# One decoder layer on one core: a carried sum folded to 64 rows, projections dealt out by step size, and three reorderings

## The chip, the core and the metric

The kernel runs on one core of a Trainium2 chip. The core has a matrix engine (TensorE, PE in the profile, with its weight loads as PEld), three engines for elementwise work (VectorE or DVE, ScalarE or ACT, GpSimd or POOL), a sync engine SP that issues most DMAs, and 16 DMA engines. Each engine works through its own queue in order; semaphores tie the queues together. The metric is the device time of one execution in microseconds (us). Before the change the median of three runs is 848.81 us, from 848.63 to 849.54.

## The reference

One layer of a decoder on 512 tokens of width 1024, all in float32: a mixer, a cross-attention into 256 memory tokens, a feed-forward, and a last normalisation.

```
h = rms_norm(x, norm_mix);  proj = h @ w_in
q, k, v, u, gate_b, gate_c, g_a, g_b = split(proj)
# stick-breaking attention, 8 heads of 64, strictly causal
z = q.k / sqrt(64)
log_fail = where(mask, log_sigmoid(-z), 0)
log_later = reverse_cumsum(log_fail) - log_fail
o_a = where(mask, exp(log_sigmoid(z) + log_later), 0) @ v
y_b = gate_b * causal_conv3(gate_c * u)
x += (sigmoid(g_a) * (o_a @ w_branch_a) + sigmoid(g_b) * (y_b @ w_branch_b)) @ w_mix_out
x += memory_cross_attention(rms_norm(x), rms_norm(mem))     # 4 heads of 256
gate, up = split(rms_norm(x) @ w_ffn_in);  x += (silu(gate) * up) @ w_ffn_out
out = rms_norm(x, norm_final)
```

## The kernel before

**Numbers.** A float32 operand is split into a high and a low part of a shorter type: ScalarE copies (casts) the value to the high part, VectorE subtracts to get the low one. A product is then three matmuls (high·high, low·high, high·low; lines 154 to 156), and a projection of one 128-wide output tile over 512 tokens is 8 x 3 = 24 matmuls of 512 columns. Its weights arrive by a DMA on SP's queue (`wr`, line 141) and are split by ScalarE (`wh`, line 149) and VectorE (`wl`, line 150).

**The stick-breaking attention.** Four pairs of heads `p` are swept; for each the key tiles `kt` go 3, 2, 1, 0, so there are 16 steps `(p, kt)`. Key tile `kt` sees the queries from `128 kt` on: 128, 256, 384 and 512 columns a head. Scores stand transposed, keys on the 128 rows. A step has three parts:

- `scores(p, kt)` (line 437) makes z on PE; ScalarE and VectorE turn it into e, the softplus of z (lines 444 to 447), which GpSimd masks with a select (line 402). `fails` splits e into `l` (lines 416, 417), adds what the key tiles above left (line 462), and queues `rests`, which splits that running sum into two tiles `r`, high and low.
- `weights(p, kt)` adds to z the running sum over all rows of the later key tiles (matmuls with `neg1`, all −1, line 480; one for each part of `r`) and the sum within the tile (matmuls with `negtri`, line 483; one for each part of `l`). ScalarE takes the exponential (`a`, line 485), GpSimd masks it (line 402), and VectorE makes `ah` and `al` (lines 489, 490).
- `values` multiplies by v (line 502) and at kt = 0 joins the two heads' halves in `ot` (lines 510, 511).

**What sets the order.** The loop over the steps (line 554) deals out a list `fill` of projections for the next pair (`qk_part`), the convolution branch (`conv`: gc, cu and gb in turn, lines 372 to 388) and the first gates, so that PE has work while the other engines make e and a. Step i issues its fills, with the scores of step i+1 in their middle, then its own `weights`, then `values` of step i−1. The number of fills of a step follows a straight line through the whole list. Each engine gets its instructions in the order in which a scheduler then lays them. Before step 9 `mem_factors` is issued: it normalises the memory tokens' factors `rm`, writes them to DRAM (`rmd`, line 534) and reads them back spread over all rows (`rmb`, line 536), both by GpSimd's DMA queue:

```
d = dpool.tile([1, MEM], F32, tag="rm", name="rmd")
nc.gpsimd.dma_start(d.rearrange("o (t p) -> p (o t)", p=P), rm)
rmb = cpool.tile([P, MEM], F32, tag="rmb", name="rmb")
nc.gpsimd.dma_start(rmb, d.broadcast_to([P, MEM]))
```

**Later stages.** The merge (lines 613 to 636) makes eight tiles `merged[m]`, each split into `mh` and `ml` (line 174); the memory keys `km` follow (lines 635 to 648), evicted by VectorE at line 642 with `rmb`. The feed-forward forms its first product from seven products of half size in each of 22 column blocks, so a use `(m, i)` is product i of block m (line 855); the list `uses` is their order on PE. Products 0, 3, 4 and 5 of a block share one PSUM bank `z`, which is read between them (`sa`, `sb`, line 876, ScalarE); product 1 has bank `v`, products 2 and 6 have `y`. `mean2` and `turn_r2` (lines 1071 to 1076) give the feed-forward's normalisation; `second` is a VectorE addition behind product 4. At the end `last_half` multiplies the last 128 rows of output, and for them `rstd(t1)`, `rstd_end(t1)` and `store` normalise and write out (lines 1274 to 1309).

PSUM has two banks for projections, four for z and two for o; all short-lived tiles (`e`, `a`, `cu`, `ot`) share eight buffers.

Of the kernel before, what the change touches and what calls it, by code (L numbers as in the profile page):

```python
# [9 lines left out]
F32R = mybir.dt.float32r  # L10
AF = mybir.ActivationFunctionType
# [32 lines left out]
def hybrid_layer(ctx: ExitStack, tc: tile.TileContext, xT_d, memT_d, mem_d, cols_d, wv_d, win_d,  # L44
# [18 lines left out]
    def nm(s):  # L63
        count[0] += 1
        return f"{s}{count[0]}"
# [102 lines left out]
    def split(src, s, scale=None, cols=512, last=()):  # L168

        hi, lo = unit(s + "h", cols), unit(s + "l", cols)  # L170
        if scale is None:
            casts.append(nc.scalar.copy(hi, src))
            after(casts[-1], last)
            nc.vector.tensor_tensor(out=lo, in0=src, in1=f(hi), op=ALU.subtract)
        else:
            nc.scalar.activation(hi, src, AF.Copy, scale=scale)
            nc.vector.scalar_tensor_tensor(out=lo, in0=src, scalar=scale, in1=f(hi),
                                           op0=ALU.mult, op1=ALU.subtract)
        return hi, lo
# [234 lines left out]
    def lsplit(t, n, tag, bufs, last=()):  # L414
        hi, lo = (lpool.tile([P, n], F32R, tag=tag, name=nm(tag), bufs=bufs) for _ in range(2))
        after(nc.scalar.copy(hi, t), last)
        nc.vector.tensor_tensor(out=lo, in0=t, in1=f(hi), op=ALU.subtract)
        return hi, lo

    def rests(p, kt, hs, e, w, last):  # L420
        rest[p, kt - 1, hs] = lsplit(e, w, f"r{kt}", 4 // len(hs), last)

    def part_of(parts, hs, some, n):

# [118 lines left out]
        fill += [(conv, p, i) for i in range(3)]  # L543
    for m in range(EARLY):
        fill += [(gate, m, 0), (gate, m, 1)]
    n_fill = len(fill)

    qk_part(0, 0)
    qk_part(0, 1)
# [4 lines left out]
    for i in range(len(steps) + 1):  # L554
        if i in MEM_AT:
            mem_square(MEM_AT.index(i))
        if i == MEAN_AT:
            rm, rmb = mem_factors()
        some = []
        while fill and (n_fill - len(fill) < (i + 1) * (n_fill - 1) / len(steps)  # L560
                        if i < len(steps) else True):
            some.append(fill.pop(0))
        if i + 1 < len(steps):
            to = lambda: scores(*steps[i + 1])
            if len(some) == 1:
# [46 lines left out]
    for m in range(KD):  # L612
        sig = []
        for j in range(2):
            if (m, j) not in gates:
                gate(m, j)
            t = gates.pop((m, j))
            sigmoid = nc.scalar.activation(t, t, AF.Sigmoid)
            after(sigmoid, exps[-2:])
            sig.append(t)  # L620
        w = load_w(wbr_d[m])
        for j in (1, 0):
            if m == 0 and j == 0:
                gate(EARLY, 0)
            ps = mmtile("br")
            gemm(ps, w, (oT, yb)[j], 4 * j)
            nc.vector.tensor_tensor(out=sig[j], in0=ps, in1=sig[j], op=ALU.mult)
        nc.vector.tensor_tensor(out=sig[0], in0=sig[0], in1=sig[1], op=ALU.add)
        merged.append(split(sig[0], "m"))
        if m == SUMS_AT:  # L630
            weight_sums(range(SUMS_FIRST), merged[m][0])
        if m % 2 == 0:
            mem_split(m // 2)
# [3 lines left out]
    for m in range(KD):  # L637
        w = load_w(wmk_d[m])
        ps = mmtile("km")
        gemm(ps[:, :MEM], w, mg)  # L640
        t = tmp("km", MEM)
        nc.vector.tensor_tensor(out=t, in0=ps[:, :MEM], in1=rmb, op=ALU.mult)
        if m % 2 == 0:
            pair = unit("kmh"), unit("kml")
        hi, lo = (u[:, (m % 2) * MEM:(m % 2 + 1) * MEM] for u in pair)
        nc.scalar.copy(hi, t)
        nc.vector.tensor_tensor(out=lo, in0=t, in1=f(hi), op=ALU.subtract)
        km.append((hi, lo))
    vm = [[None] * 2 for _ in range(MT)]
    for n in range(2):  # L650
        pss = [ztile("vm") for _ in range(MT)]
# [254 lines left out]
                n1 = acts[j][1][:, :HS]  # L906
                nc.vector.tensor_tensor(out=n1, in0=acts[j][0][:, :HS], in1=n1, op=ALU.subtract)

    uses = [(0, 0), (0, 1), (0, 2)]
    for m in range(NF):  # L910
        if m < NF - 2:
            uses += [(m, 3), (m + 1, 0), (m, 4), (m + 1, 1), (m, 5), (m + 1, 2), (m, 6)]
        elif m == NF - 2:
            uses += [(m, 3), (m + 1, 0), (m, 4), (m + 1, 1), (m + 1, 2), (m + 1, 3), (m, 5),
                     (m + 1, 4), (m, 6), (m + 1, 5), (m + 1, 6)]
# [135 lines left out]
    with tc.manual_schedule(engines={mybir.EngineType.PE, mybir.EngineType.Activation,  # L1051
# [6 lines left out]
        for n, (m, i) in enumerate(uses):  # L1058
            if (m, i) == (1, 0):
                product(banks[m]["z"], m, i, range(KP - 1, KP))  # L1060
            elif n > 2:
                product(bank_of(m, i), m, i)
            if i == 4:
                reads(m, i)
            else:
                if i == 1 and m > 0:
                    second(m - 1)
                reads(m, i)
            if n + AHEAD < len(uses):
                ffn_form(*uses[n + AHEAD])  # L1070
            if n + AHEAD + SUM_AHEAD < len(uses):
                ffn_raw(*uses[n + AHEAD + SUM_AHEAD])
            if (m, i) == (1, 1):
                mean2 = mean2()
            elif (m, i) == (0, 6):
                r2b[0] = mean2[0]("r0b", bank=mmtile)
                turn_r2()

            if i == 0 and m > 1:
                evict(m - 2, 0)  # L1080
            elif i == 4 and 0 < m < NF - 1:
                evict(m - 1, 1)
            elif i == 1 and m > 1:
                evict(m - 2, 2)
            if (m, i) == (NF - 2, 6):
                w, x3 = out_cast(*w23(0)), half_form(3, 0, 0)
                evict(m, 0)
                evict(m, 1)
                rest_of(*x3)
                x2 = half_form(2, 1, 0)  # L1090
            if (m, i) == (NF - 1, 5):
                evict(NF - 2, 2)
                rest_of(*w)
                rest_of(*x2)
                n2_of(x2[0], 1)
                x3 = half_form(3, 1, 0)
            if n == len(uses) - 6:
                w, x = out_cast(*w01(0)), cast_first(0)
                rest_of(*w)
                rest_of(*x)  # L1100
            elif (m, i) == (NF - 1, 4):
                w, x = out_cast(*w01(1)), cast_first(1)
                x2 = half_form(2, 0, 0)
                second(NF - 1)
                rest_of(*w)
                rest_of(*x)
                rest_of(*x2)
                n2_of(x2[0], 0)
# [165 lines left out]
        def rstd(ts):  # L1274


            a, b = ss[:, :TT][:, ts], ss[:, TT:][:, ts]
            if ts == t1:
                nc.vector.tensor_scalar(out=var[:, ts], in0=b, scalar1=a, scalar2=s1b, op0=ALU.add,
                                        op1=ALU.add)  # L1280
            else:
                nc.vector.tensor_tensor(out=var[:, ts], in0=a, in1=b, op=ALU.add)
            after(nc.scalar.activation(ry[:, ts], var[:, ts], AF.Ln, bias=eps_t), tables)
            nc.scalar.activation(ry[:, ts], ry[:, ts], AF.Exp, scale=-0.5)
            nc.vector.tensor_scalar(out=rv[:, ts], in0=var[:, ts], scalar1=EPS, scalar2=None,
                                    op0=ALU.add)

        def rstd_end(ts):

# [11 lines left out]
        def store(t, h, how):  # L1301
            y, r = ys[t, h], ra[:, t:t + 1]
            if how == "act":
                nc.scalar.activation(y, y, AF.Copy, scale=r)
            else:
                nc.vector.scalar_tensor_tensor(out=y, in0=y, scalar=r, in1=gain[h], op0=ALU.mult,
                                               op1=ALU.mult)
            q = nc.scalar if (t, h) == (1, 0) else nc.sync
            q.dma_start(out[t * P:(t + 1) * P, h * 512:(h + 1) * 512], y)

        def last_half(c):
            bank = ztile("p5b")
# [23 lines left out]
        rstd_end(t0)  # L1336
        half()
        store(0, 0, "act")
        half = last_half(1)
        store(0, 1, "both")  # L1340
        half()
        rstd(t1)
        rstd_end(t1)
        store(1, 1, "both")
        store(1, 0, "act")


_OUT = ((512, 1024), 'float32')
# [61 lines left out]
```

## Time and profile before

| what | us |
|---|---|
| median of three runs | 848.81 (848.63 to 849.54) |
| the profiled execution, its own time | 848.86 |
| its span, first to last instruction | 847.2 |
| PE busy | 837.0 |
| VectorE busy | 654.0 |
| ScalarE busy | 453.3 |
| GpSimd busy | 158.9 |

The page divides the span into busy time of each engine; the chain that ended last follows the work back from the last instruction; the list of waits says which engine stood idle for whom; and the timeline gives single instructions with their start, their duration and, in brackets, the idle time before them and what ended it. Matmuls overlap: one of 512 columns is shown as 390 ns, though the next starts after some 227, so distances between starts are what counts on PE. In a row, `out<-in` names the tiles, and `xN` counts instructions that the view has merged.

### The profile page before, as it was taken

To read this page: it belongs to the slowest core of one execution; us is meant where nothing else is said; L and a number is where in the kernel's file an instruction comes from. 1 tells how busy PE (TensorE), PEld (TensorE's weight loads), DVE (VectorE), ACT (ScalarE), POOL (GpSimd) and SP (SyncE) were. 2 spreads that over 40 slices of the span, in tenths; PEclk is the share of its full clock that TensorE was granted. 3 is DMA by queue.
4 is the path that set the end of the run, shared out by engine and by line. 5 is a ranking of instruction groups with operands and counts; after the bars stand their busy time and mean duration, and the time that the engine had idled before them with its cause. 6 is when DMAs were issued, how large, how long until landed. Compare 5 with 4: busy or idle time off the path is not lost.

```text
span 847.2 us, 12667 instructions
## 1 busy us (share of the span) xinstructions
PE 837.0 (99%) x4779; PEld 737.9 (87%) x4779; DVE 654.0 (77%) x1036; ACT 453.3 (54%) x806; POOL 158.9 (19%) x165
## 2 busy tenths in 40 slices
PE   9999999999999999999999999999999999999996
PEld 7888887888888899888888789999999999988885
DVE  7878978895757686588455689888888778899886
ACT  7576766574333344443444556655555555666654
POOL 0011121220556660163000001111111110000401
PEclk9999999999999999999999999999999999999999
DMA  8552454225588776466431425767767773465552
GB/s 299 158 159 100 131 103 97 80 78 188 195 306 306 268 267 200 171 227 250 152 83 50 111 74 144 177 179 182 191 177 187 190 186 86 149 223 200 179 182 99
DMA packets 51214, 143.72 MB, mean 170 GB/s; under 512 B 5745, under 2 KB 6769, under 8 KB 48338
## 3 DMA queue, kind: packets, MB, share of 16 engines
q1 hardware_dynamic: 41506, 107.89, 38.5%
q0 software_dynamic: 9360, 34.75, 15.7%
q8 instruction: 37, 0.61, 0.3%
q10 hardware_dynamic: 288, 0.28, 0.1%
q14 instruction: 23, 0.19, 0.1%
HBM read 125.20 MB, written 13.64 MB: 164 GB/s over the span
## 4 chain that ended last, share of the span: by engine, by line
PE 95%; DVE 2%; ACT 1%; issue 1%; POOL 0%; POOLq 0%; DVEq 0%; ACTq 0%
PE z L855 15%; PE p L1124 12%; PE y L855 7%; PE pr L154 7%; PE pr L155 7%; PE pr L156 7%; PE v L855 4%; PE r L155 3%; PE r L154 3%; PE r L156 3%; PE v L272 3%; PE mq L156 2%; PE mq L154 2%; PE mq L155 2%; PE br L156 2%; PE br L155 2%
## 5 line engine op out<-in xcount | busy, mean ns | idle before, releaser
L149 ACT CAST wh<-wr 128x1024 fp32r<-128x1024 f32 x84 | 88.0, 1051 | 156.5 <-issue 65.5
L150 DVE TENSOR_TENSOR wl<-wr,wh 128x1024 fp32r<-128x1024 f32 x84 | 112.4, 1340 | 36.5 <-ACT wh L149 35.9
L154 PE MATMUL pr<-xgh,wh 128*128 128x512 f32 x288 | 112.9, 392 | 0.1
L155 PE MATMUL pr<-xgl,wh 128*128 128x512 f32 x288 | 112.4, 390 | 0.0
L156 PE MATMUL pr<-xgh,wl 128*128 128x512 f32 x288 | 112.2, 390 | 0.0
L589 POOL TENSOR_TENSOR pre<-pre 128x512 f32<-128x512 f32 x44 | 73.7, 1679 | 31.7 <-DMA pre<-in_w_ffn_out_dram 29.4
L824 POOL DMA_DIRECT2D ws<-in_w_ffn_in_dram x22 | 26.6, 1210 | 256.1 <-DVE wf L845 120.2
L855 PE MATMUL z<-xdh,wf 128*128 128x256 f32 x352 | 70.4, 283 | 0.0
L156 PEld LDWEIGHTS pr<-xgh,wl 128*128 128x128 f32 x288 | 54.1, 188 | 11.5
L154 PEld LDWEIGHTS pr<-xgh,wh 128*128 128x128 f32 x288 | 54.1, 188 | 10.9 <-DVE gc L372 0.3
L155 PEld LDWEIGHTS pr<-xgl,wh 128*128 128x128 f32 x288 | 54.1, 188 | 10.5
L876 ACT COPY sa<-z 128x256 f32<-128x256 f32 x44 | 16.4, 372 | 79.2 <-PE z L855 79.1
L855 PEld LDWEIGHTS z<-xdh,wf 128*128 128x128 f32 x352 | 58.0, 192 | 0.0
L845 DVE TENSOR_TENSOR wf<-s,wf 128x512 fp32r<-128x512 f32 x44 | 30.3, 690 | 25.9 <-ACT wf L844 25.7
L855 PE MATMUL z<-xdl,wf 128*128 128x256 f32 x176 | 49.8, 283 | 0.0
L936 DVE TENSOR_TENSOR wl<-wr,wh 128x1024 fp32r<-128x1024 f32 x33 | 41.0, 1243 | 4.7 <-ACT wh L1003 4.7
L1003 ACT CAST wh<-wr 128x1024 fp32r<-128x1024 f32 x33 | 34.6, 1049 | 5.5 <-PE xt L1209 2.8
L855 PE MATMUL z<-xch,wf 128*128 128x256 f32 x176 | 35.4, 284 | 0.1
L855 PE MATMUL v<-xoh,wf 128*128 128x256 f32 x176 | 35.4, 283 | 0.0
L855 PE MATMUL y<-xch,wf 128*128 128x256 f32 x176 | 35.4, 283 | 0.0
L855 PE MATMUL z<-xf,wf 128*128 128x256 f32 x264 | 35.4, 283 | 0.0
L855 PE MATMUL y<-xoh,wf 128*128 128x256 f32 x176 | 35.3, 283 | 0.0
(341 smaller groups left out, 2391.8 us busy)
## 6 DMA issues: line engine op xcount, KB each, us to landing
wr<-in_w_in_dram SPq DMA_DIRECT2D x36, 512.0 KB, 3.3
pre<-in_w_ffn_out_dram POOLq DMA_DIRECT2D x11, 1024.0 KB, 8.0
sums<-pre POOLq DMA_DIRECT2D x11, 1024.0 KB, 5.0
ws<-in_w_ffn_in_dram SPq DMA_DIRECT2D x22, 512.0 KB, 3.7
wg<-in_w_ffn_in_dram SPq DMA_DIRECT2D x22, 512.0 KB, 4.3
ws<-in_w_ffn_in_dram POOLq DMA_DIRECT2D x22, 512.0 KB, 6.3
wr<-sums SPq DMA_DIRECT2D x22, 512.0 KB, 3.8
wr<-in_w_ffn_out_dram SPq DMA_DIRECT2D x16, 512.0 KB, 3.8
```

The source lines that it names most:

```text
L149: after(nc.scalar.copy(h2, raw), lead[-1:])
L150: lows.append(nc.vector.tensor_tensor(out=l2, in0=raw, in1=f(h2), op=ALU.subtract))
L154: nc.tensor.matmul(ps, a[0], b[0], start=start, stop=False, **kw)
L155: nc.tensor.matmul(ps, a[0], b[1], start=False, stop=False, **kw)
L156: nc.tensor.matmul(ps, a[1], b[0], start=False, stop=stop, **kw)
L589: nc.gpsimd.tensor_tensor(out=t[:, a, :], in0=t[:, a, :], in1=t[:, b, :], op=ALU.add)
L824: nc.gpsimd.dma_start(s13, a[:, 0:4:3, :], accum_op=ALU.add)
L845: nc.vector.tensor_tensor(out=w[:, 1, :], in0=raw, in1=f(w[:, 0, :]), op=ALU.subtract)
L855: nc.tensor.matmul(ps[:, :HS], a, b, start=i < 3 and k == 0 and j == 0, stop=k == KP - 1 and j == 2, skip_group_check=True)
L936: nc.vector.tensor_tensor(out=lo, in0=src, in1=f(hi), op=ALU.subtract)
L1003: nc.scalar.copy(hi, raw)
L1124: nc.tensor.matmul(res[i][s2], a[:, ts], b, start=j == 0 and n == 0, stop=n == 2 and j == (BEHIND - 1 if (i, s2) == (5, 1) else NJ - 1))
```

## The change

Six edits:

1. `rests` no longer splits the running sum into two tiles of 128 rows. It adds the upper 64 rows to the lower 64 (ScalarE copies the upper half to a temporary's lower rows, VectorE adds), and puts the high part of the result into rows 0 to 63 of one tile and the low part into rows 64 to 127. `weights` then needs one matmul with `neg1` instead of two.
2. The loop deals two fills to each step with kt = 1 and one to each other step, and the rest at the end.
3. The split of the last merged tile is issued behind the eviction of `km[0]`.
4. The first uses of the feed-forward come in another order; `second(0)`, `mean2` and `turn_r2` move with them.
5. For the last 128 rows Ln takes the last partial sum of squares `s1b` as its input and the rest as its bias, so the sum isn't formed first.
6. The last two stores are issued from a function of their own: ScalarE's half first, VectorE's half in two pieces.

```diff
     def rests(p, kt, hs, e, w, last):
-        rest[p, kt - 1, hs] = lsplit(e, w, f"r{kt}", 4 // len(hs), last)
+        low, high = HALVES
+        t = tmp("rf")[:, :w]
+        after(nc.scalar.copy(t[low, :], e[high, :]), last)
+        nc.vector.tensor_tensor(out=t[low, :], in0=t[low, :], in1=e[low, :], op=ALU.add)
+        r = lpool.tile([P, w], F32R, tag=f"r{kt}", name=nm("r"), bufs=2 // len(hs))
+        nc.scalar.copy(r[low, :], t[low, :])
+        nc.vector.tensor_tensor(out=r[high, :], in0=t[low, :], in1=f(r[low, :]), op=ALU.subtract)
+        rest[p, kt - 1, hs] = r,
...
-        while fill and (n_fill - len(fill) < (i + 1) * (n_fill - 1) / len(steps)
-                        if i < len(steps) else True):
+        while fill and (i == len(steps) or len(some) < (2 if steps[i][1] == 1 else 1)):
             some.append(fill.pop(0))
...
-        merged.append(split(sig[0], "m"))
+        if m < KD - 1:
+            merged.append(split(sig[0], "m"))
...
         km.append((hi, lo))
+        if m == 0:
+            merged.append(split(sig[0], "m"))
...
-    uses = [(0, 0), (0, 1), (0, 2)]
-    for m in range(NF):
+    uses = [(0, 0), (0, 1), (0, 2), (0, 3), (1, 0), (1, 1), (0, 4), (1, 2), (0, 5), (0, 6)]
+    for m in range(1, NF):
...
-                if i == 1 and m > 0:
+                if i == (2 if m == 1 else 1) and m > 0:
                     second(m - 1)
...
-            if (m, i) == (1, 1):
+            if (m, i) == (0, 5):
                 mean2 = mean2()
-            elif (m, i) == (0, 6):
+            elif (m, i) == (1, 3):
...
+        def rstd_begun(ts):
+            nc.vector.tensor_scalar(out=var[:, ts], in0=ss[:, :TT][:, ts],
+                                    scalar1=ss[:, TT:][:, ts], scalar2=EPS, op0=ALU.add,
+                                    op1=ALU.add)
+
+        def rstd_of_rest(ts):
+            nc.scalar.activation(ry[:, ts], s1b, AF.Ln, bias=var[:, ts])
+            nc.scalar.activation(ry[:, ts], ry[:, ts], AF.Exp, scale=-0.5)
+            nc.vector.tensor_tensor(out=rv[:, ts], in0=var[:, ts], in1=s1b, op=ALU.add)
...
+        def store_last(t):
+            r = ra[:, t:t + 1]
+            rows = out[t * P:(t + 1) * P, :]
+            nc.scalar.activation(ys[t, 0], ys[t, 0], AF.Copy, scale=r)
+            nc.scalar.dma_start(rows[:, :512], ys[t, 0])
+            for c in range(2):
+                cs = slice(c * HS, (c + 1) * HS)
+                y = ys[t, 1][:, cs]
+                nc.vector.scalar_tensor_tensor(out=y, in0=y, scalar=r, in1=gain[1][:, cs],
+                                               op0=ALU.mult, op1=ALU.mult)
+                nc.sync.dma_start(rows[:, 512 + c * HS:512 + (c + 1) * HS], y)
...
+        rstd_begun(t1)
         half = last_half(1)
         store(0, 1, "both")
         half()
-        rstd(t1)
+        rstd_of_rest(t1)
         rstd_end(t1)
-        store(1, 1, "both")
-        store(1, 0, "act")
+        store_last(1)
```

In the changed kernel the lines of `weights` are 8 higher (480 is 488, 483 is 491, 502 is 510, 534 is 542, 536 is 544).

**PE, step 9, weights(2,2).** Its rows before: scores of the next step, then a whole projection (`pr314`, 24 matmuls, of which the first two and the last are shown), then the matmuls with the carried `l3` and with `l2` into bank `z282`, then values.

```order
L437 MATMUL z308_1421<-qk187_889,qk205_969 128x384
L154 MATMUL pr314_1442<-xgh21_153,wh312_1438 128x512
L155 MATMUL pr314_1442<-xgl22_154,wh312_1438 128x512
...
L156 MATMUL pr314_1442<-xgh47_218,wl313_1439 128x512
L480 MATMUL z282_1305<-l3272_1270,neg1_91 128x2x128
L480 MATMUL z282_1305<-l3273_1271,neg1_91 128x2x128
L483 MATMUL z282_1305<-l2291_1352,negtri_95 128x512
L483 MATMUL z282_1305<-l2292_1353,negtri_95 128x512
L502 MATMUL o320_1483<-ah286_1335,v63_351 128x128
```

The same place in the changed kernel: the scores stand in the middle of the one projection that is left in this step (`pr305`, the last 12 of its 24 matmuls follow, the first and the last of them are shown).

```order
L445 MATMUL z307_1413<-qk187_891,qk205_971 128x384
L154 MATMUL pr305_1397<-xgh35_188,wh303_1393 128x512
...
L156 MATMUL pr305_1397<-xgh47_218,wl304_1394 128x512
L488 MATMUL z282_1309<-l3272_1274,neg1_91 128x2x128
L488 MATMUL z282_1309<-l3273_1275,neg1_91 128x2x128
L491 MATMUL z282_1309<-l2291_1356,negtri_95 128x512
L491 MATMUL z282_1309<-l2292_1357,negtri_95 128x512
L510 MATMUL o314_1453<-ah286_1339,v63_351 128x128
```

The projection `pr314` has moved behind weights(2,2).

**POOL and VectorE at the same place, in the changed kernel.** First GpSimd: the write of `rm`, the mask of the scores' e, the reading back, the mask of a of the step before, and the next masks.

```order
L542 DMA rmd_1387<-rm301_1380 128x2x1
L402 AFFINE_SELECT e283_1314<-e283_1314 128x2x128
L544 DMA rmb_1389<-rmd_1387 128x256
L402 AFFINE_SELECT a285_1336<-a285_1336 128x256
L402 AFFINE_SELECT a311_1446<-a311_1446 128x2x128
```

Up to the fourth of these rows nothing has moved against before; the fifth then stood two masks later. VectorE behind that mask of a (`a285`), up to `l2292`, which the second matmul L491 above reads, and on to the new add of the fold (`rf296`):

```order
L497 TENSOR_SCALAR ah286_1339<-a285_1336,r071_372 128x256
L519 TENSOR_TENSOR ot288_1347<-o221_1048,ot288_1347 64x512
L498 SCALAR_TENSOR_TENSOR al287_1340<-a285_1336,r071_372,ah286_1339 128x256
L519 TENSOR_TENSOR ot288_1347<-o222_1049,ot288_1347 64x512
L417 TENSOR_TENSOR l2292_1357<-e283_1314,l2291_1356 128x512
L470 TENSOR_TENSOR e283_1314<-e283_1314,e264_1230 128x2x128
L174 TENSOR_TENSOR ol290_1353<-ot288_1347,oh289_1352 128x512
L336 TENSOR_TENSOR qk294_1362<-qk284_1332,qk293_1361 128x512
L425 TENSOR_TENSOR rf296_1369<-rf296_1369,e283_1314 64x512
```

The first five of these rows stand in the same order as before.

**VectorE, the last merged tile.** Before, with `ml` ahead of the eviction of the first `km`:

```order
L150 TENSOR_TENSOR wl616_3010<-wr614_3007,wh615_3009 128x1024
L174 TENSOR_TENSOR ml594_2895<-g582_2822,mh593_2894 128x512
L642 TENSOR_TENSOR km599_2929<-km598_2904,rmb_1383 128x256
L150 TENSOR_TENSOR wl621_3045<-wr619_3042,wh620_3044 128x1024
L647 TENSOR_TENSOR kml601_2932<-km599_2929,kmh600_2931 128x256
```

and in the changed kernel:

```order
L150 TENSOR_TENSOR wl616_3018<-wr614_3015,wh615_3017 128x1024
L649 TENSOR_TENSOR km597_2933<-km596_2908,rmb_1389 128x256
L150 TENSOR_TENSOR wl621_3053<-wr619_3050,wh620_3052 128x1024
L654 TENSOR_TENSOR kml599_2936<-km597_2933,kmh598_2935 128x256
L174 TENSOR_TENSOR ml601_2940<-g582_2830,mh600_2939 128x512
```

The split `ml` has moved behind the eviction, the next weights' subtract and the split of `km`.

More of the change, by code (lines that the diff above doesn't have):

```diff
@@ L545, in hybrid_layer @@
         fill += [(gate, m, 0), (gate, m, 1)]
-    n_fill = len(fill)
     qk_part(0, 0)
@@ L1277, in rstd @@
             a, b = ss[:, :TT][:, ts], ss[:, TT:][:, ts]
[L1278 to L1282, printed above, removed]
+            nc.vector.tensor_tensor(out=var[:, ts], in0=a, in1=b, op=ALU.add)
             after(nc.scalar.activation(ry[:, ts], var[:, ts], AF.Ln, bias=eps_t), tables)
@@ L1307, in store @@
                                                op1=ALU.mult)
-            q = nc.scalar if (t, h) == (1, 0) else nc.sync
-            q.dma_start(out[t * P:(t + 1) * P, h * 512:(h + 1) * 512], y)
+            nc.sync.dma_start(out[t * P:(t + 1) * P, h * 512:(h + 1) * 512], y)
+        def store_last(t):
[9 more added lines that the diff above has]
+                nc.sync.dma_start(rows[:, 512 + c * HS:512 + (c + 1) * HS], y)
         def last_half(c):
```

## The prediction

> **What bounds the kernel now.** I read the page's busy shares first, then the chain that ended last, then what TensorE waited for.
>
> ```profile
> PE 837.0 (99%) x4779; PEld 737.9 (87%) x4779; DVE 654.0 (77%) x1036; ACT 453.3 (54%) x806; POOL 158.9 (19%) x165
> PE 95%; DVE 2%; ACT 1%; issue 1%; POOL 0%; POOLq 0%; DVEq 0%; ACTq 0%
> PE warm L232 <- DVE neg L91: 1.4, 1, 1.4
> PE z L437 <- ACT a L485: 0.9, 1, 0.9
> PE km L154 <- DVE km L642: 0.3, 1, 0.3
> 731.03 62.59 PE p L1124 x276
> ```
>
> TensorE (PE) is the bound: 837.0 of 847.2 us, 95% of the chain, and only three waits of note. So two kinds of edit can pay: fewer matmul columns, and the removal of a wait of PE itself. Any wait that the change adds to PE counts in full. The last row gives the true rate: 276 matmuls of 512 columns in 62.59 us, **0.227 us each** (a matmul's own duration overlaps the next), so a projection of 24 takes 5.44 us. Everything below is by start to start.
>
> **Folded rests.** In each head pair, 2 of 4 neg1 matmuls of 256 columns and 2 of 4 of 384 columns go. Their groups, and PE's timeline where they stand:
>
> ```profile
> L480 PE MATMUL z<-r,neg 128*128 128x384 f32 x16 | 4.1, 335 | 0.0
> L480 PE MATMUL z<-r,neg 128*128 128x256 f32 x16 | 3.2, 279 | 0.0
> ...
> 134.57 0.40 PE L480 MATMUL z<-l,neg 128*128 128x256 f32 x2
> 134.80 0.62 PE L483 MATMUL z<-l,negtri 128*128 128x512 f32 x2
> ...
> 151.24 0.51 PE L480 MATMUL z<-r,neg 128*128 128x384 f32 x2
> 151.58 0.62 PE L483 MATMUL z<-l,negtri 128*128 128x512 f32 x2
> ```
>
> Two of 256 columns occupy 134.80 − 134.57 = 0.23 us, two of 384 columns 151.58 − 151.24 = 0.34 us. Half of each sixteen goes: 4 x 0.23 + 4 x 0.34 = **−2.28 us**. In exchange each of 12 rests gets one ScalarE copy and one VectorE add more, on 64 rows.
>
> ```profile
> L511 DVE TENSOR_TENSOR ot<-o,ot 64x512 f32<-64x512 f32 x8 | 5.5, 685 | 0.1
> ```
>
> 64 rows cost what 128 rows do (685 ns here, 0.69 us for 128 rows of L417 further down), so nothing is saved on the halved subtract. With 0.69 us for 512 columns and about 0.56 for 384 (an estimate halfway to the 0.43 of 256 columns, the row at 132.93) a pair gets 0.69 + 2 x 0.56 = 1.8 us more on VectorE. This lies beside PE except where VectorE has no slack; see below. The way from e to r grows from two operations to four (1.3 to 2.6 us); r is read a step later, behind at least one projection of 5.44 us, and that is the cover. Without it a pair would lose up to 1.3 us.
>
> **Fills dealt out anew.** The projections keep their order; what moves is where the attention steps stand among them. Fills come in twos at steps 2, 6, 10 and 14 instead of 3, 6, 9 and 12. At pair 2 that moves one projection of 24 matmuls, with its weight load, cast and subtract, from ahead of weights(2,2) to behind it. In pairs 0, 1 and 3 one projection moves too, by a step; no transfer to DRAM stands in a queue there and PE waits nowhere in them, so I put them at nothing (up to +0.5). PE's old stalls in pair 2:
>
> ```profile
> 135.54 0.27 PE L502 MATMUL o<-al,v 128*128 128x128 f32 x1
> 135.94 0.50 PE L154 MATMUL pr<-xgh,wh 128*128 128x512 f32 x1
> ...
> 146.63 0.39 PE L156 MATMUL pr<-xgh,wl 128*128 128x512 f32 x1
> 147.95 0.66 PE L437 MATMUL z<-qk,qk 128*128 128x128 f32 x4 [0.93 <-ACT a L485]
> ```
>
> The first is 135.94 − 135.54 − 0.11 = 0.29 us (a bank that VectorE's gc freed), the second 147.95 − 146.63 − 0.23 = 1.09 us. With a projection more in front of each, both go: **−1.38 us**. What is late next is at weights(2,2), and it is no arithmetic but a DMA on GpSimd's queue:
>
> ```profile
> 120.01 0.74 POOL L534 DMA_DIRECT2D rmd<-rm  x1 [3.39 <-DVE rm L129]
> ...
> 129.07 0.57 POOL L536 DMA_DIRECT2D rmb<-rmd  x1 [6.69 <-DMA rmd<-rm]
> ...
> 130.11 0.35 DVE L489 TENSOR_SCALAR ah<-a,r 128x256 fp32r<-128x256 f32 x1 [6.08 <-POOL a L402]
> ...
> 132.20 0.69 DVE L417 TENSOR_TENSOR l<-e,l 128x512 fp32r<-128x512 f32 x1
> 132.93 0.43 DVE L462 TENSOR_TENSOR e<-e,e 128x256 f32<-128x256 f32 x1
> ```
>
> These are the timelines of POOL and VectorE (start, duration, idle before and its releaser in brackets). The memory factors go to DRAM and back. POOL holds the second transfer until the first has landed, 8.8 us after its issue; behind it stands the select of a, behind that on VectorE ah, ot, al, ot and then l, ready at 132.20 + 0.69 = 132.89. That l feeds the second L483 matmul of weights(2,2). Today PE comes there at 134.80 + 0.23 = 135.03, with 2.1 us to spare: the 6-us wait is free. With a projection less ahead PE comes at 135.03 − 5.44 = 129.59. These engines' orders there are unchanged, and the transfer's start hangs on step 8, which the dealing shifts together with PE. So PE, with its whole stream behind it, waits 132.89 − 129.59, and 0.06 for the hand-over (as at 135.94, after gc's end at 135.88): **+3.4 us**. The unknown is the landing, which I bound by the nearest transfers (rows of the DMA view, of the page and of single windows, and one of POOL's timeline):
>
> ```profile
> rmd<-rm POOLq DMA_DIRECT2D x1, 1.0 KB, 8.8
> ...
> wr<-in_w_in_dram SPq DMA_DIRECT2D x36, 512.0 KB, 3.3
> ...
> 531.69 0.79 POOL L212 DMA_DIRECT2D rt<-row  x1 [2.83 <-DMA row<-r0b]
> ...
> wr<-in_w_in_dram SPq DMA_DIRECT2D x1, 512.0 KB, 8.7
> ```
>
> A row of 2 KB written on the same queue held POOL up for 2.83 us after its issue, where rmd took 129.07 − 120.75 = 8.3; with 2.83 l would be ready at about 127.4, before PE comes, and the term is 0. That is the lower end; a landing later than today's adds to the 3.4 one for one, and no row shows one over 10 us here. For 8.8 us speaks the last row, from the issues between 123 and 126 us: a weight load on SP's queue, issued at that time, took 8.7 us against the page's 3.3. Memory answered everyone late, just while the 1 KB was under way, and the timing around it stays. I take 8.8.
>
> [...]
>
> Behind the release VectorE is the next to be late:
>
> ```profile
> 132.90:154.00 21.10, 21.00 (x37) 1.00 0.30 94
> ...
> 151.29 0.68 DVE L417 TENSOR_TENSOR l<-e,l 128x512 fp32r<-128x512 f32 x1
> ```
>
> It is busy 21.00 of 21.10 us, up to the l of step (2,0), done at 151.97. From 132.93 that is 19.04 us, with the three new adds 20.8; for two new waits on ScalarE (the fold's second copy, and a) I take 0.6, between 0 and 1.4: ready at 154.4. PE has, from 135.03 to its use near 152.60, 17.57 − 1.38 of stalls − 0.57 of folded matmuls + 5.44 of the projection = 21.06 us, and arrives at 132.95 + 21.06 = 154.0: **+0.4 us** (0 to 1.2).
>
> **Last merged tile.**
>
> ```profile
> 308.50 1.78 DVE L174 TENSOR_TENSOR ml<-g,mh 128x512 fp32r<-128x512 f32 x1
> ...
> 310.13 0.28 PE L156 MATMUL km<-mgh,wl 128*128 128x256 f32 x1
> 310.76 0.36 PE L154 MATMUL km<-mgh,wh 128*128 128x256 f32 x1 [0.34 <-DVE km L642]
> ```
>
> VectorE's 1.78-us split stands ahead of km's eviction (L642), and PE stands from 310.25 to 310.76. With the eviction first: **−0.5 us** (−0.3 if the now later split delays the next eviction).
>
> **Entry of the feed-forward.** PE starts the product (0,4) late, since its bank is being copied:
>
> ```profile
> 515.14 0.52 PE L855 MATMUL z<-xf,wf 128*128 128x256 f32 x3
> 515.34 0.37 ACT L876 COPY sa<-z 128x256 f32<-128x256 f32 x1 [0.24 <-PE z L855]
> 515.77 0.39 PE L855 MATMUL z<-xch,wf 128*128 128x256 f32 x1
> ```
>
> 515.77 − 515.14 − 3 x 0.12 = 0.27 us. Now a product on another bank (12 matmuls, 1.4 us) lies between and covers the 0.37-us copy: **−0.27 us**, give or take 0.3, since the mean's reads and the second sum stand nearer to their users.
>
> **End.**
>
> ```profile
> 841.04 0.27 DVE L1279 TENSOR_SCALAR rms<-ss,s1b 128x1 f32<-128x1 f32 x1
> 841.34 0.29 ACT L1283 ACTIVATE rms<-rms,eps_t 128x1 f32<-128x1 f32 x1 [0.34 <-DVE rms L1279]
> ...
> 843.16 0.37 ACTq L1309 DMA_DIRECT2D out_dram<-l  x1
> ```
>
> Ln takes the sum as its input and no longer waits for L1279: up to 0.3 us. The last VectorE store is cut in two, but ScalarE's store, issued at 843.16, is as late and stays whole: nothing there. One DMA more against that: **−0.3 us** (−0.1 to −0.5).
>
> **Sum**: −2.28 − 1.38 + 3.4 + 0.4 − 0.5 − 0.27 − 0.3 = −0.9 us. The profiled execution took 848.86 us (span 847.2, 1.7 around it), 0.05 over the median 848.81 of the runs; both lead to **847.9 us**. By the bounds of the terms this case reaches from 846.8 to 849.0.
>
> **Rivals.**
> 1. *The landing is quick, no new wait.* Without the +3.4 and what follows it (+0.4): 844.1 us. For it: the 2.83 us at 531.69. Against: the weight load caught in the same delay.
> 2. *VectorE becomes the bound in pair 2.* The new copies and adds cost their upper bound, 1.2 instead of 0.4: 848.7 us; the fold then does little of what its count of matmuls says. Against it: VectorE idles 6.08 us just before, so no backlog is carried in.
> 3. *The other side: PE's pause lets its clock fall.*
>
> ```profile
> 1.37 3.73 PE L232 MATMUL warm<-neg 128*128 128x512 f32 x8 [1.37 <-DVE neg L91]
> ...
> 841.20:844.50 3.30, 0.00 (x0) 0.00 (x0) 1.44 (x5) 1.22 (x3) 0.00 (x0) 1.00 0.55 213
> 844.60:847.10 2.50, 0.00 (x0) 0.00 (x0) 0.00 (x0) 0.00 (x0) 0.00 (x0) 0.50 0.32 123
> ```
>
> The windows give the granted clock third from the end. After the last matmul (over by 839.95) it is still 1.00 up to 844.5 and 0.50 from 844.6: a pause of 4.6 us has brought it down. At the start 8 matmuls at the low clock took 3.73 us against 8 x 0.227 = 1.82, a loss of 1.9. So it is certain from a landing 1.2 us later than today's on: 847.9 + 1.2 + 1.9 = 851.0 us, slower than before. Against it: the bound on the landing. Between a pause of 3.4 us and one of 4.6 the end of the kernel doesn't tell where the clock falls; should it fall at 3.4 already, with the landing as today, the time is 847.9 + 1.9 = 849.8 us.
>
> [...]
>
> **How the numbers follow.** Forecast 0.63, rival 1 0.18, rival 2 0.10, rival 3 0.05 with the late landing and 0.04 without. A measurement of this kernel tells about 0.2% (1.7 us) from no change: faster is below 847.1, slower above 850.5. Faster: rival 1 and 0.12 from the forecast's own range, 0.30. Slower: rival 3's late landing and 0.01, 0.06. Same: the rest, 0.64. The range takes in rival 1 with some 0.3 below it, rival 2 and the forecast, from 843.8 to 849.2, and leaves out rival 3; the forecast's own range is 846.8 to 849.0.
>
> **What would show it.** In the profile after: one PE wait of about 3.4 us at the second matmul of weights(2,2), released by VectorE's l, and behind it POOL's wait of 6 to 7 us for rmd (if POOL waits 3 us, rival 1); no waits for a, for km's eviction or for the copied bank; 16 matmuls fewer with neg1; PE's granted clock 1.00 after the pause (else rival 3); Ln starting with its sum, 0.3 us earlier. The prediction falls if rmd lands early, or if the steps around weights(2,2) reach PE in another order than today's.

## The result, and the profile after

The changed kernel takes 851.31 us (median of 8 runs, 849.97 to 852.31), the kernel before 848.50 us in the runs beside it: ratio 1.0033, 95% interval 1.0022 to 1.0044. It is slower, where 847.9 and a range up to 849.2 had been forecast. The profiled execution took 852.17 us, its span is 850.3 us.

Busy times, the chain that ended last, and TensorE's waits, of the changed kernel:

```profile
PE 837.4 (98%) x4763; PEld 737.8 (87%) x4763; DVE 657.2 (77%) x1049; ACT 459.4 (54%) x818; POOL 158.0 (19%) x165
PE 93%; DVE 4%; DMA 1%; ACT 1%; issue 0%; POOL 0%; DVEq 0%; POOLq 0%
PE z L491 <- DVE l L417: 4.0, 1, 4.0
PE warm L232 <- DVE neg L91: 1.4, 1, 1.4
PE br L154 <- DVE g L353: 0.4, 1, 0.4
```

The 16 matmuls are gone (4763 against 4779), and so are the two old waits, for a and for km. At their head stands the wait that had been forecast. Yet PE is busier by 0.4 us with fewer matmuls, so some of them ran longer. Timelines of GpSimd and TensorE show both:

```profile
119.72 0.73 POOL L542 DMA_DIRECT2D rmd<-rm  x1 [3.62 <-DVE rm L129]
...
129.04 0.57 POOL L544 DMA_DIRECT2D rmb<-rmd  x1 [7.57 <-DMA rmd<-rm]
...
128.51 0.39 PE L491 MATMUL z<-l,negtri 128*128 128x512 f32 x1
132.92 0.79 PE L491 MATMUL z<-l,negtri 128*128 128x512 f32 x1 [4.03 <-DVE l L417]
...
138.63 0.59 PE L155 MATMUL pr<-xgl,wh 128*128 128x512 f32 x1
139.06 0.41 PE L156 MATMUL pr<-xgh,wl 128*128 128x512 f32 x1
139.30 0.40 PE L154 MATMUL pr<-xgh,wh 128*128 128x512 f32 x1
```

GpSimd waits for the landing of rmd until 129.04, as before (129.07). TensorE has done its first L491 matmul by 128.51 + 0.23 = 128.74 and starts the second at 132.92, a pause of 4.2 us. Behind it matmuls of 512 columns start 0.43 us apart (139.06 − 138.63) instead of 0.227, up to 139.06. The windows (length, busy time of PE, PEld, DVE, ACT and POOL, then the granted clock, the DMA share and GB/s) name the reason:

```profile
129.00:132.00 3.00, 0.00 (x0) 0.00 (x0) 1.89 (x4) 0.00 (x0) 0.99 (x2) 1.00 0.66 160
132.00:132.90 0.90, 0.00 (x0) 0.00 (x0) 0.84 (x2) 0.72 (x2) 0.00 (x0) 0.63 0.59 153
132.90:138.00 5.10, 5.08 (x14) 4.21 (x15) 4.48 (x8) 5.03 (x11) 0.65 (x2) 0.50 0.34 76
...
139.00:140.00 1.00, 1.00 (x6) 0.77 (x5) 1.00 (x3) 0.52 (x1) 0.44 (x1) 0.97 0.00 0
```

The granted clock falls to half while TensorE pauses: a mean of 0.63 over 0.9 us means 0.67 us at 0.50, so it fell at 132.23. It is back at about 139.06, 6.8 us later. Of those, TensorE works 6.14 us, from 132.92 to 139.06. In them it starts a matmul of 512 columns, four of 128 and eleven of 512, for which the full clock needs 12 x 0.227 + 4 x 0.11 = 3.16 (0.11 is 135.54 − 135.43, two starts of 128 columns in the kernel before). The low clock costs **2.98 us**.

So in this profile: pause +4.2, low clock +3.0, fold −2.3, old stalls of pair 2 −1.4, entry of the feed-forward −0.3: +3.2 us, and the span grew by 3.1.

### The profile page after: what moved, and what is told of

Read it like the earlier page. It is cut to its first block, busy times and chain, and to the rows that moved or that the text cites. A ratio compares the mean times of both kernels' runs of the same rounds, so it can differ in the third digit from the quotient of the medians.

```text
span 850.3 us, 12669 instructions
## 1 busy us (share of the span) xinstructions
PE 837.4 (98%) x4763; PEld 737.8 (87%) x4763; DVE 657.2 (77%) x1049; ACT 459.4 (54%) x818; POOL 158.0 (19%) x165
## 4 chain that ended last, share of the span: by engine, by line
PE 93%; DVE 4%; DMA 1%; ACT 1%; issue 0%; POOL 0%; DVEq 0%; POOLq 0%
PE z L864 15%; PE p L1133 12%; PE y L864 7%; PE pr L154 6%; PE pr L155 6%; PE pr L156 6%; PE v L864 4%; PE r L155 3%; PE r L154 3%; PE r L156 3%; PE v L272 3%; PE mq L156 2%; PE mq L154 2%; PE mq L155 2%; PE br L154 2%; PE br L155 2%
```

## The experiments

Theory A: GpSimd's queue, blocked by the landing of rmd, makes TensorE pause at weights(2,2), and the pause halves its clock. Rivals: the fold overloads VectorE (B), or the clock fell for another reason (C). Every ratio is to the kernel before, run beside it on the same chip.

**Take the block away.** The reading back of the factors goes three steps later on GpSimd's queue; nothing else is touched.

```diff
-        nc.gpsimd.dma_start(rmb, d.broadcast_to([P, MEM]))
-        return rm, rmb
+        return rm, rmb, lambda *last: after(nc.gpsimd.dma_start(rmb, d.broadcast_to([P, MEM])), last)
...
-            rm, rmb = mem_factors()
+            rm, rmb, spread = mem_factors()
+        if i == MEAN_AT + 3:
+            spread(*exps[-1:])
```

> The changed kernel, with only the reading back of the memory factors (rmb) issued three steps later on GpSimd's queue; their write to DRAM (rmd) stays where it is. Theory A (GpSimd's queue, blocked by the landing of rmd, makes TensorE pause 4.2 us at weights(2,2), and the pause halves its clock for 6 us): both go, 851.3 - 4.2 - 2.9 = 844.2 us, with up to 1 us of other waits in pair 2; the landing of rmd still takes 8 to 9 us, and nobody waits for it. Rival B (the fold's extra copies and adds make VectorE the bound in pair 2, and the wait only shows that): the wait moves to another reader of VectorE's tiles, and the time stays at 848 us or more.

Measured: 844.15 us, ratio 0.9950 (0.9937 to 0.9962). All of TensorE's waits in the list, GpSimd's two transfers, and two windows around the old pause:

```profile
PE warm L232 <- DVE neg L91: 1.4, 1, 1.4
...
119.50 0.73 POOL L542 DMA_DIRECT2D rmd<-rm  x1 [3.62 <-DVE rm L129]
...
149.40 0.57 POOL L544 DMA_DIRECT2D rmb<-rmd  x1
...
128.00:134.00 6.00, 6.00 (x31) 5.03 (x31) 5.39 (x9) 4.57 (x9) 1.39 (x3) 1.00 0.51 127
134.00:140.00 6.00, 6.00 (x28) 4.99 (x27) 5.90 (x12) 5.03 (x10) 0.00 (x0) 1.00 0.35 111
```

Only the wait at the start is left; TensorE is busy throughout at full clock, and rmb is issued without waiting. The medians differ by 851.31 − 844.15 = 7.2 us, as much as the pause and the low clock together (4.2 + 3.0); the two profiled spans differ by 7.9, since a wait of 0.5 us in the merge (see the smaller terms below) is gone too. Theory A holds, and rival B falls for the new dealing. It is also a version that beats both kernels.

**Keep the wait, fill the pause.** Matmuls with a zero stationary tile go into the bank between the two L491.

```diff
-            for part in sp[p, kt, hs]:
+            for j, part in enumerate(sp[p, kt, hs]):
+                for _ in range(14 if (p, kt, j) == (2, 2, 1) else 0):
+                    nc.tensor.matmul(z, zero1, sp[p, kt, hs][0], start=False, stop=True,
+                                     skip_group_check=True)
                 nc.tensor.matmul(z, negtri, part, start=False, stop=True, skip_group_check=True)
```

> The changed kernel, with 14 matmuls of a zero weight tile (they add nothing to the bank) between the two L491 matmuls of weights(2,2), so that TensorE works through 3.2 us of its wait. Theory A: the wait for l ends at the same time, the granted clock stays at 1.00, and only the 2.9 us of the half clock go: 851.3 - 2.9 = 848.4 us. Rival C (the clock falls for a reason other than TensorE's pause): it is 0.50 from 132 to 139 us again, 851.3 us.

> The changed kernel with 7 instead of 14 matmuls of a zero weight tile in the wait at weights(2,2): 1.6 us of the wait are filled, 2.6 us of pause are left. With 14 (1.1 us left) the clock stayed at 1.00, and the 2.9 us won there came back as 1.7 us of waits for VectorE's l. Theory F (any pause over some 2 us can halve the clock, since part of an idle stretch is enough): 0.50 for 3.4 or 6.8 us, 851.3 us. Rival G (a window of 3.4 us must be idle nearly throughout): the clock stays at 1.00, 850.8 us.

With 14: 850.80 us (850.50 to 851.62, ratio 1.0027, 1.0016 to 1.0037). Window, and TensorE's waits, which are then for VectorE's l:

```profile
134.00:140.00 6.00, 6.00 (x28) 4.98 (x27) 4.81 (x7) 5.16 (x12) 0.86 (x3) 1.00 0.33 73
...
PE z L497 <- DVE l L420: 1.9, 3, 0.9
...
150.06 0.66 PE L448 MATMUL z<-qk,qk 128*128 128x128 f32 x4 [0.21 <-ACT a L499]
...
154.34 0.50 PE L497 MATMUL z<-l,negtri 128*128 128x512 f32 x1 [0.43 <-DVE l L420]
...
155.80 0.50 PE L497 MATMUL z<-l,negtri 128*128 128x512 f32 x1 [0.55 <-DVE l L420]
```

The clock stays at 1.00, so rival C falls: the fall hangs on the pause. But 0.5 us are won, not 2.9. TensorE at full clock comes sooner to tiles that are not ready. VectorE has worked without a break since 140.1 us (after two gaps of 0.5 and 0.8 us), and TensorE pays there: by distances between starts 0.4 us at 150.06 (where it waits for ScalarE's a), 0.6 at 154.34 and 0.7 at 155.80. In the changed kernel the low clock had hidden this backlog. There the last of these l and the matmuls behind it stand so:

```profile
153.94 0.68 DVE L417 TENSOR_TENSOR l<-e,l 128x512 fp32r<-128x512 f32 x1
...
156.50 0.63 PE L491 MATMUL z<-l,negtri 128*128 128x512 f32 x2
```

This l is ready at 154.62, and the second of the matmuls, which reads it, starts at 156.73. That leaves 2.1 us to spare, less than the 3.0 by which TensorE would come sooner at full clock.

With 7, which leave 133.33 − 129.08 − 7 x 0.227 = 2.7 us of pause, the four runs fall into two kinds: 850.32 and 850.52 us with a mean granted clock of 0.999 and 0.996, 852.81 and 853.29 with 0.993. The profiled one is the first of them and shows no fall:

```profile
129.08 1.77 PE L495 MATMUL z<-l,zero 128*128 128x512 f32 x7
133.33 0.50 PE L497 MATMUL z<-l,negtri 128*128 128x512 f32 x1 [2.48 <-DVE l L420]
```

6.8 us at half of 850 lower the mean by 0.004, which fits the second kind. Neither of its runs was profiled, and 0.996 is a little less than any run without a pause shows (0.997 to 0.999). So as far as the mean clock tells, this version halves the clock in some executions and not in others; theory F and rival G each had a half of it, and the last section sets TensorE's work against the clock. One thing stays open: the second kind takes 2.6 us more than the first, and 1.4 more than the changed kernel's six runs of low mean clock (851.6 on average), though a low clock that hides the backlog should leave it near these.

**Take the dealing alone, and leave it out alone.** The hunk of the loop is the only difference, in one direction or the other:

```diff
-        while fill and (i == len(steps) or len(some) < (2 if steps[i][1] == 1 else 1)):
+        while fill and (n_fill - len(fill) < (i + 1) * (n_fill - 1) / len(steps)
+                        if i < len(steps) else True):
```

> The kernel before with the new dealing as the only edit. Theory A: the wait at weights(2,2) stands again, but shorter than in the changed kernel (4.2 us), since without the folds of pairs 0 and 1 TensorE comes about 0.9 us later: 3.3 to 3.5 us. The old stalls of pair 2 (1.4 us) go. What it tells apart: if a pause of 3.4 us leaves the clock at 1.00, 848.5 - 1.4 + 3.4 + 0.4 = 850.9 us; if it halves it, another 2.9 us, 853.8 us. Rival B (no fold here, so VectorE isn't overloaded): 847.1 us.

> The changed kernel with the old dealing of the fills; the other five edits stay. Theory A: TensorE reaches weights(2,2) a projection (5.4 us) later and waits for nothing there; the fold gives its 2.3 us, the entry of the feed-forward 0.3 and the end 0.1, the old stalls of pair 2 (1.4 us in all) may stay: 848.5 - 2.7 = 845.8 us, between 844.8 and 846.5. Rival B: the fold costs more than it gives, 848.5 us or more.

The dealing alone: 853.65 us (853.12 to 854.82), ratio 1.0058 (1.0044 to 1.0072). TensorE's timeline and two windows of it:

```profile
130.19 0.39 PE L483 MATMUL z<-l,negtri 128*128 128x512 f32 x1
133.62 0.80 PE L483 MATMUL z<-l,negtri 128*128 128x512 f32 x1 [3.05 <-DVE l L417]
...
133.00:133.60 0.60, 0.00 (x0) 0.00 (x0) 0.57 (x1) 0.60 (x2) 0.00 (x0) 0.60 1.02 164
133.60:139.00 5.40, 5.38 (x15) 4.41 (x16) 4.79 (x9) 5.40 (x12) 0.91 (x3) 0.50 0.34 77
```

This answers the question that the prediction had left at a chance of 0.04: here the pause is 133.62 − 130.19 − 0.23 = **3.2 us**, and the clock falls all the same. Its five runs have mean clocks of 0.994 and 0.995.

The changed kernel with the old dealing: 849.69 us, ratio 1.0016 (1.0007 to 1.0024), and not 845.8. No pause stands at weights(2,2), but other waits do:

```profile
136.18 0.50 PE L154 MATMUL pr<-xgh,wh 128*128 128x512 f32 x1 [0.58 <-DVE gc L372]
139.96 0.73 PE L445 MATMUL z<-qk,qk 128*128 128x512 f32 x2 [0.30 <-ACT a L493]
149.31 0.66 PE L445 MATMUL z<-qk,qk 128*128 128x128 f32 x4 [1.50 <-ACT a L493]
...
PE z L491 <- DVE l L417: 0.7, 2, 0.5
```

By distances between starts they are 0.7, 0.5 and 1.7 us in pair 2 and twice some 0.5 for l in pair 3, 3.9 us together against 1.4 before: the fold's gain is given back. That looked like rival B, or like the old stalls grown. The next three runs tell them apart.

**The same corners without the block.**

> The kernel before, with the reading back of the memory factors three steps later as the only edit: none of the change's own edits. Theory A2 (the same block on GpSimd's queue made the old stalls of pair 2: VectorE idles for 6 us behind it, then carries its work as a backlog, which made the stalls of 0.3 and 1.1 us): both stalls go, 848.5 - 1.4 = 847.1 us. Rival D (those stalls belong to the old dealing, which gives these steps too little cover): they stay, 848.5 us.

> The kernel before with the new dealing and the late reading back, so the dealing alone without the block. Theory A2: as with the old dealing and the late reading back, 847.1 us. Rival D: the dealing takes the two old stalls away by itself, so this is 847.1 us, and the kernel before with the late reading back stays at 848.5 us; the two runs together tell.

> The changed kernel with the old dealing and with the late reading back. With the old dealing alone it took 849.7 us, and TensorE waited 3.9 us in pairs 2 and 3. Theory A2: these waits are the backlog behind GpSimd's block; without the block they go, 844.2 to 844.9 us, as with the new dealing, which is then worth nothing by itself. Rival E (the fold's extra copies and adds overload ScalarE and VectorE where the old dealing puts the steps close together): the waits stay, 848.5 to 849.7 us.

| median us | as it is | with the late reading back |
|---|---|---|
| before | 848.6 | 847.61 (ratio 0.9989, 0.9980 to 0.9998) |
| before + new dealing | 853.65 | 847.75 (0.9986, 0.9977 to 0.9995) |
| changed, old dealing | 849.69 | 846.23 (0.9971, 0.9960 to 0.9982) |
| changed | 851.31 | 844.15 (0.9950, 0.9937 to 0.9962) |

Without the block the kernel before loses its wait for a. Its list of waits then holds only these:

```profile
PE warm L232 <- DVE neg L91: 1.4, 1, 1.4
PE km L154 <- DVE km L643: 0.3, 1, 0.3
```

The gain is 1.0 us where 1.4 were expected. So the two old stalls of pair 2 were the backlog behind GpSimd's block and not a fault of the dealing. Rival D falls. The new dealing by itself is then worth nothing (847.61 and 847.75). With the old dealing the fold keeps only its waits in pair 3:

```profile
PE warm L232 <- DVE neg L91: 1.4, 1, 1.4
PE z L491 <- DVE l L417: 0.7, 2, 0.5
PE br L154 <- DVE g L353: 0.2, 1, 0.2
```

846.23 lies between theory A2 (844.2 to 844.9) and rival E (848.5 and up). Both have a share: 849.69 − 846.23 = 3.5 us were the block's, and 846.23 − 844.15 = 2.1 us are what the new dealing is worth with the fold, of which the two waits for l in pair 3 make about 1.0 and the wait for g in the merge 0.3; for the rest no wait was found.

**The landing itself.** In the fast version, the factors are written once more at step 12 in the same form, and 1 KB from one row at step 14.

```diff
+            after(nc.gpsimd.dma_start(dpool.tile([1, MEM], F32, tag='rm2', name='rme')
+                                      .rearrange('o (t p) -> p (o t)', p=P), rm), last)
...
+        if i == MEAN_AT + 5:
+            after(nc.gpsimd.dma_start(dpool.tile([1, MEM], F32, tag='rm3', name='rmf'),
+                                      r0b[0:1, :MEM]), exps[-1:])
```

> The fast version (changed kernel with late reading back) with two more small writes to DRAM on GpSimd's queue, which nobody reads: step 12 writes the same factors once more in the same form (256 single elements from 128 rows, 1 KB), step 14 writes 1 KB from one row in one piece. Theory H (the landing of 8.6 to 9.1 us seen in all profiles is that of the scattered form): the second scattered write takes 8 to 9 us too, the row 2 to 3 us. Rival I (memory is late at the place of rmd for another reason): both land in 2 to 4 us.

One execution, the DMA view's issues (KB, us from issue to landing):

```profile
rmd<-rm POOLq DMA_DIRECT2D x1, 1.0 KB, 8.8
rme<-rm POOLq DMA_DIRECT2D x1, 1.0 KB, 9.1
rmf<-r0b POOLq DMA_DIRECT2D x1, 1.0 KB, 2.3
```

The same size on the same queue lands in 2.3 us from one row and in 9.1 us from 128 rows of two elements, 32 us after the first. The DMA engines were busy for 0.87 of rmd's time in the kernel before (8.8 us, 120.0 to 128.8), and for 0.28 of that of the second scattered write here (9.1 us, 151.9 to 161.0), so their load doesn't explain the delay either. Theory H holds: here the delay belongs to the scattered form (8.8 and 9.1 us at two places), not to the place.

## Why the prediction was wrong

**Right, and shown by runs.** The wait: its place, its waiter, its releaser and the landing behind it (8.8 forecast; 9.0 in the changed kernel, 8.6 to 9.1 in nine profiles). The gain without it: 844.1 us was worked out for the case of a quick landing, and 844.15 is what the kernel takes once nobody waits for it. The fold with the last four edits: −2.28 − 0.5 − 0.27 − 0.3 = −3.4 forecast, 847.75 − 844.15 = 3.6 measured, without the block. That this sum agrees so well is in part luck, since two of its terms did not come as forecast (see the smaller terms).

**The step that failed** is the clock. The forecast's sum kept TensorE at full clock through its pause and had no term for a fall. Rival 3 held the fall for "certain from a landing 1.2 us later than today's on" and gave it a chance of 0.04 with the landing as today. That chance was my estimate. The only fall that the profile before showed came 4.6 us after the last matmul, and I took that for the length that a pause needs. It was only one sample. The clock fell in the profiles of the changed kernel (a pause of 4.2 us) and of the dealing alone (3.2). By the mean clock (0.993 to 0.995 for a fall, 0.997 and more for none) it fell in six of the changed kernel's eight runs, in all five of the dealing alone, in two of the four with 7 matmuls in the pause and in none of the seven with 14 (a pause of 1.1). One run each of the changed kernel and of the version with 7 has 0.996, and the mean can't place it.

The time of rival 3 without the late landing, 849.8 us, was also too small in its terms:

- The low clock costs 3.0 us of matmul time, not 1.9. I had priced it by the eight matmuls at the start of the kernel (3.73 us). In the middle it stays low for 6.8 us, of which 6.1 fall on work.
- The pause is 4.2 us, not 3.4. TensorE comes at 128.74, not 129.59: the folds of pairs 0 and 1 shorten its way by 2 x 0.57 = 1.1 us, while the landing moved by 0.03 only. I counted the fold's gain and forgot that it takes TensorE sooner to a point that doesn't move. The dealing alone bears that out: without the folds the pause is 3.2.

With these two, the forecast's other terms give 847.9 + 0.8 + 3.0 = 851.7, less 0.4 for the next point. That 851.31 was measured is closer than it deserves: this sum still holds 0.5 for the merged tile and 0.2 at the end that were not won, and the median is over runs with and without a fall. Rival 3's 851.0 for a late landing came near by luck, since the landing wasn't late.

**Without the fall** the forecast would have missed as well. The version with 14 matmuls in the pause keeps the full clock and takes 850.80 us, outside the range to 849.2: the pause is 0.8 longer, and the backlog behind it costs 1.7 instead of 0.4.

**VectorE's backlog**, +0.4 us: nothing in the changed kernel, since the low clock gave VectorE the time to catch up; 1.7 us where the pause is filled, 0.4 of it for ScalarE's a. The mechanism is there, and the term was too small.

**The old stalls of pair 2**, −1.38 us: they went, but not, as the prediction put it, for "a projection more in front of each". They also go with the old dealing, once the block is gone, and they were children of the very wait that was called free.

**The landing's evidence.** The prediction took row<-r0b for the lower end of what rmd can take. But that is 2 KB of one row, and rmd is 256 elements from 128 rows; the last experiment shows that this is the difference (2.3 us for 1 KB of one row, 9.1 for the same size in the scattered form). So the quick row wasn't a bound for rmd at all, and rival 1 deserved less than its 0.18. Nor is busy memory needed for it, which the prediction read from the late weight load: with the DMA engines much less busy (0.28 against 0.87) the scattered write took as long (9.1 us against 8.8).

**Smaller terms.** The entry of the feed-forward came as forecast: the 0.27-us wait at (0,4) stands in the profile of the kernel before (515.77) and not in that of the changed kernel, where TensorE works through from 515.14 to 519.95. The last merged tile did not show its 0.5: the wait for km is gone, but one of 0.5 us has come in the merge, 12 matmuls ahead of the first km. VectorE's g is late there, behind two mgl that took 3.37 us while GpSimd added for most of the time:

```profile
303.59 4.97 POOL L595 TENSOR_TENSOR pre<-pre 128x512 f32<-128x512 f32 x3
...
301.82 3.37 DVE L612 SCALAR_TENSOR_TENSOR mgl<-mk,gcol,mgh 128x256 fp32r<-128x256 f32 x2
305.11 0.68 DVE L353 TENSOR_TENSOR g<-pr,r0b 128x512 f32<-128x512 f32 x1
...
305.84 0.50 PE L154 MATMUL br<-oh,wh 128*128 128x512 f32 x1 [0.37 <-DVE g L353]
```

In the kernel before with dealing and late reading back, which lacks this edit, neither wait occurs; in the kernel before, where g isn't waited for, the two mgl take 2.95 us; in the changed kernel with the late reading back neither wait occurs either. Which of them comes may depend on where GpSimd's additions fall, which was not tested; what the edit is worth stays open. The end gave 0.1 us instead of 0.3: from the last matmul to the end of the span it was 7.2 us before and is 7.1 now. ScalarE's last store is issued 846.09 − 842.90 = 3.19 us after the last matmul's start, before 843.16 − 839.66 = 3.50; SP's second piece, issued behind the first, follows it:

```profile
842.90 0.28 PE L1347 MATMUL p5b<-wq,f45l 128*128 128x256 f32 x1
...
845.86 0.81 SPq L1339 DMA_DIRECT2D out_dram<-u  x2
846.09 0.35 ACTq L1333 DMA_DIRECT2D out_dram<-l  x1
```

Where the 0.3 us won there were lost was not tried.

## What to carry to other kernels

A wait that costs nothing today is a debt on somebody's slack: before moving work away from in front of it, list what each queue holds there, and first move the waiting instruction (here one DMA, three steps later) out of the queue. What is saved on the bound engine ahead of a fixed time comes back as a wait at it: here 1.1 us of folds, and a pause of 4.2 us instead of 3.2. And price a pause of the matrix engine with its clock as well: here pauses of 3.2 and 4.2 us halved it in the profiles, and after the longer one the slower matmuls cost another 3.0 us. Price the engines behind it too: when the clock alone was kept up, 0.5 of the 3.0 came back, and 1.7 went to waits for tiles that weren't ready.

## What the runs showed of the hardware

The granted clock stays at half for 6.8 us in both profiles that show a fall inside the kernel: from 132.23 to 139.06, and in the dealing alone from 133.12 (0.60 over 0.6 us) to about 139.94. By the traces' records of the granted clock, the low stretch of the changed kernel lasts 6.827 us, and full speed lasts 126.29 us before the fall in both profiles, 706.56 and 709.97 behind it, and 839.68 in the kernel before. These are 37, 207, 208 and 246 times 3.413 us, half of the low stretch: in these traces the changes stand on a grid of 3.413 us. Where it lies against the kernel differs between the profiles: the first rise of the clock comes 4.9 us after the start in the kernel before, 5.9 in the changed kernel and 6.8 in the dealing alone.

So the work in one stretch of the grid can be set against the clock behind it. In the first four of these rows the clock falls behind the stretch, in the others it does not:

| profile | stretch of 3.41 us | TensorE busy in it, us | clock behind it |
|---|---|---|---|
| changed kernel, the pause | 128.82 to 132.23 | 0.07 | 0.50 |
| dealing alone, the pause | 129.71 to 133.12 | 0.86 | 0.50 |
| changed kernel, its end | 842.21 to 845.62 | 0.97 | 0.50 |
| changed, old dealing, its end | 840.11 to 843.52 | 1.23 | 0.50 |
| changed, 7 matmuls in the pause | 129.33 to 132.74 | 1.52 | 1.00 |
| changed, old dealing and late reading back, its end | 835.09 to 838.50 | 1.88 | 1.00 |
| kernel before, its end | 837.76 to 841.17 | 2.18 | 1.00 |

In these rows the clock falls behind the stretches with 1.23 us of work or less and stays at 1.00 behind those with 1.52 or more. From the first rise to the last matmul, the other stretches of the kernel before hold 2.49 us or more, and those of the changed kernel 2.73 or more, and the clock falls behind none of them. This was read from the traces and not tried by an experiment of its own. It fits the 4.6 us that misled the prediction: the stretch in which the last matmul of the kernel before ended still held 2.18 us of work, and the fall came behind the next, which held none. Of the two pauses that halved the clock, 3.34 and 2.55 us lay in one stretch (3.41 − 0.07 and 3.41 − 0.86), and 1.89 (3.41 − 1.52) with 7 matmuls, where it stayed. An estimate from these rows: if 2.2 us in one stretch (3.41 − 1.23) are enough, a pause of 3.4 us has them in some 7 cases in 10, should the grid lie at random, and not in the 0.04 of the prediction. By the same count a pause of 4.2 us should nearly always halve the clock, yet one of the changed kernel's eight runs has a mean of 0.997; it was not profiled, so how long its pause was isn't known. On the way back, in the changed kernel, a stretch with 2.73 us of work (132.23 to 135.65) did not lift the clock, and the next, which was full (3.41), did.

And the writes of 1 KB to DRAM in 256 separate elements from 128 rows took 8.6 to 9.1 us, about four times as long as the one row of the same size (2.3).
